# Queries and keys projected as features by tokens, and constants of the late loads derived past the values

## The chip, the cores and the metric

One core of one Trainium2 chip runs the whole block: TensorE (PE) multiplies into PSUM, VectorE (DVE) and the scalar engine (ACT) compute on SBUF and PSUM, GpSimd (POOL) on SBUF alone, and DMAs are issued from the queues of SyncE (SP) and ACT. The metric is device time in microseconds (us).

## The reference

A hybrid decoder block on x of 512 tokens by 1024. The part that matters here:

```python
xn = _rms_norm(h, mix_norm[l])
proj = xn @ w_in[l]                    # q, k, v, indexer, RWKV and gate columns
q = _rms_norm(q.reshape(B, S, 8, 64), attn_q_norm[l])
k = _rms_norm(k.reshape(B, S, 8, 64), attn_k_norm[l])
# sparse attention, by blocks of 128 queries:
scores = einsum(relu(einsum(q_idx, k_idx)), w_idx)       # then causal mask
_, sel = lax.top_k(scores, 128)
logits = einsum(q, k[sel]) * 64 ** -0.5 + rel_bias[bucket(q_pos - sel)]
y_attn = softmax(logits) @ v[sel]
```

Beside it run an RWKV-7 branch on other columns of the same projection, two gates, an output projection and a SwiGLU channel mixer.

## The kernel before

Every weight matrix comes in as one stream of chunks of 128x1024, 512 KB each, in the order of use. `chunk` (L233) loads one from SP's queue (w_raw, 2 buffers), ACT rounds it to the matmul's format (w_hi, L241, 3 buffers) and the rest, raw - hi, is made by GpSimd, or for every third chunk from number 17 on by VectorE (w_lo, L245, 3 buffers). A dense product is three matmuls (hi x hi, hi x lo, lo x hi), so that it keeps float32's precision.

`products` is the dense work from the first projection to the end: indexer's keys and queries, then queries, keys and values, RWKV's columns, gates, output, channel mixer. In its middle:

```python
for gain, name in ((qg, "q"), (pc("kn"), "k")):
    for g in range(2):
        yield from dense_k(xn, lambda t, ps: head_rms(g, gain, name, t, ps))
```

`dense_k` gives tokens by features: 128 tokens x 256 columns (four heads) to a product of 256 columns, two token blocks to a PSUM bank (ps_d, 3 banks). `head_rms` takes one such block out of PSUM (qraw), squares it (both ACT), sums by head (L449), adds epsilon (L450, both VectorE), raises to -1/2 on GpSimd (qrs, L452) and multiplies (L453, VectorE). Its `rest`, 14.5 modelled us later, flips the block to features by tokens (ps_i, 2 banks, L169) and takes it out as a high half (ACT, L464) and a low half (VectorE, L465): queries have the high half of a head on 64 partitions and the low half on the other 64 of one tile (qs_); keys have the high half twice (kh_, L467) and the low half twice (kl_, L468), so that two matmuls give the logits.

While that runs, VectorE does the indexer: `scores` (24 score products, ps_c, 3 banks; relu on ACT, weighted sum L416 and L420) and `select`, which finds the 128 largest scores of a row in 16 rounds of eight for each of three query blocks (L432 finds the maxima, L433 removes them, L435 makes the mask). `attention` starts when the values are there (vt, L966); for each of 32 units (4 query blocks x 8 heads) it makes logits (L523 to L533), their exponential (ACT, L534), flips them, and multiplies by the values.

The order on TensorE is the order in which the program is written. `Streams` sets it: each part is a generator, `mm` and `flip` advance a clock by a modelled time, a part yields how long it wants to wait (the table L), and the part of lowest rank that is due goes on; the dense work has the last rank. The other engines' order is chosen by the compiler's scheduler from dependences and its own model of time. In every engine, what waits holds back all that is queued behind it.

`derive` (L358) makes small constants on VectorE after the first projection is written: multiples of parameters, rkb (from con, which is loaded late from SP's queue), and eye16 and lev1 (from level1_t, loaded late too), which only the RWKV branch reads.

## Time and profile before

| | |
|---|---|
| Time, median of 3 runs (range) | 963.98 us (963.55 to 964.72) |
| The profiled execution's own time, and its span | 964.03 us, 962.2 us |
| Mean granted clock of TensorE over the span | 0.978 |
| TensorE busy, and weight loads | 915.0 us (95%), 779.0 us (81%) |
| VectorE, scalar engine, GpSimd busy | 435.9 (45%), 350.6 (36%), 372.3 us (39%) |
| Chain that ended last, by engine | PE 84%, DVE 11%, issue 2%, ACT 1%, POOL 1% |
| HBM read, written | 74.53 MB, 2.38 MB |

Times in the rows below count from the span's start. Matmuls are pipelined: the time from the start of one to the start of the next is its pace, and its own duration is longer. A busy share over the whole span is a mean over stages that have different limits.

### The profile page before, as it was taken

Reading aid. Unit: us, or ns where it says so; the run is one execution under the profiler, and the core shown is the slowest. Engines: PE = TensorE matmul, PEld = TensorE weight load, DVE = VectorE, ACT = ScalarE, POOL = GpSimd, SP = SyncE. Lnnn points to the kernel's source line nnn. Section 1 sums busy time; section 2 is a strip of 40 time slices with the busy share of each in tenths; the row PEclk is TensorE's granted clock in tenths of the full one; section 3 lists DMA queues with packets and bytes.
Section 4 is the critical chain, followed back from the end, with each engine's and each line's share of the span. In section 5 each row is a group of like instructions: output and inputs, shape, how many; then the busy total and the mean of one; then the engine's idle time right before and its main releaser. Section 6 shows DMA issues by size and latency. Waiting matters only on the chain.

```text
span 962.2 us, 13991 instructions
## 1 busy us (share of the span) xinstructions
PE 915.0 (95%) x5670; PEld 779.0 (81%) x5670; DVE 435.9 (45%) x847; ACT 350.6 (36%) x596; POOL 372.3 (39%) x253
## 2 busy tenths in 40 slices
PE   6998777999999999999997999999999999999998
PEld 4997776888777778787886899888888888888886
DVE  5289999677466635765533715211111111101111
ACT  5454466544453433333323424332232323212120
POOL 6445441101357334444413733344444444432321
PEclk9998888999998999999998999999999999999999
DMA  6321232211212121011042222332223323223331
GB/s 230 80 89 44 67 88 66 66 45 44 77 45 66 44 81 53 24 45 44 23 143 77 88 88 69 95 100 88 99 98 92 106 88 110 88 95 102 132 110 44
DMA packets 24033, 77.80 MB, mean 81 GB/s; under 512 B 2726, under 2 KB 4223, under 8 KB 23969
## 3 DMA queue, kind: packets, MB, share of 16 engines
q1 hardware_dynamic: 20832, 72.56, 23.4%
q10 hardware_dynamic: 3136, 4.36, 1.6%
q8 instruction: 44, 0.72, 0.3%
q14 instruction: 21, 0.16, 0.1%
HBM read 74.53 MB, written 2.38 MB: 80 GB/s over the span
## 4 chain that ended last, share of the span: by engine, by line
PE 84%; DVE 11%; issue 2%; ACT 1%; POOL 1%; DMA 0%; ACTq 0%; DVEq 0%; POOLq 0%
PE ps_d L162 60%; PE ps_c L162 11%; PE ps_i L162 10%; DVE score L433 2%; PE ps_c L169 2%; DVE max L432 2%; DVE qraw L453 1%; DVE score L420 1%; DVE qs L465 1%; PE ps_i L169 1%; DVE qss L449 1%; DVE lg L527 1%; POOL w_lo L245 0%; DVE kl L465 0%; DVE xs L330 0%
## 5 line engine op out<-in xcount | busy, mean ns | idle before, releaser
L245 POOL TENSOR_TENSOR w_lo<-w_raw,w_hi 128x1024 fp32r<-128x1024 f32 (+1 forms) x94 | 222.0, 2364 | 387.5 <-ACT w_hi L241 383.9
L241 ACT ACTIVATE w_hi<-w_raw 128x1024 fp32r<-128x1024 f32 x129 | 136.6, 1059 | 346.5 <-PE ps_d L162 219.4
L162 PE MATMUL ps_d<-hnl,w_hi 128*128 128x512 f32 (+1 forms) x368 | 139.9, 380 | 0.4 <-DVE hnl L338 0.4
L162 PE MATMUL ps_d<-hnh,w_hi 128*128 128x512 f32 (+1 forms) x368 | 139.9, 380 | 0.0
L162 PE MATMUL ps_d<-hnh,w_lo 128*128 128x512 f32 (+1 forms) x368 | 139.8, 380 | 0.0
L162 PE MATMUL ps_d<-xnh,w_hi 128*128 128x512 f32 (+2 forms) x296 | 124.5, 420 | 0.0
L162 PE MATMUL ps_d<-xnh,w_lo 128*128 128x512 f32 (+2 forms) x296 | 112.8, 381 | 0.0
L162 PE MATMUL ps_d<-xnl,w_hi 128*128 128x512 f32 (+2 forms) x296 | 112.4, 380 | 0.0
L245 DVE TENSOR_TENSOR w_lo<-w_raw,w_hi 128x1024 fp32r<-128x1024 f32 x37 | 47.6, 1286 | 126.8 <-ACT w_hi L241 126.2
L1045 DVE TENSOR_TENSOR gsig<-ps_d,gsig 128x512 f32<-128x512 f32 x22 | 15.2, 692 | 157.6 <-PE ps_d L162 156.9
L162 PEld LDWEIGHTS ps_d<-hnl,w_hi 128*128 128x128 f32 x368 | 69.2, 188 | 13.4 <-DVE hnl L338 0.6
L162 PEld LDWEIGHTS ps_d<-hnh,w_lo 128*128 128x128 f32 x368 | 69.2, 188 | 13.2
L162 PEld LDWEIGHTS ps_d<-hnh,w_hi 128*128 128x128 f32 x368 | 69.2, 188 | 13.2
L162 PEld LDWEIGHTS ps_d<-xnh,w_hi 128*128 128x128 f32 x296 | 57.2, 193 | 10.0 <-issue 2.6
L162 PEld LDWEIGHTS ps_d<-xnh,w_lo 128*128 128x128 f32 x296 | 56.8, 192 | 10.5
L162 PEld LDWEIGHTS ps_d<-xnl,w_hi 128*128 128x128 f32 x296 | 57.2, 193 | 8.1 <-issue 1.9
L162 PE MATMUL ps_d<-w_hi,xnh 128*128 128x256 f32 x192 | 58.9, 307 | 0.0
L162 PE MATMUL ps_d<-w_lo,xnh 128*128 128x256 f32 x192 | 57.7, 301 | 0.0
L162 PE MATMUL ps_d<-w_hi,xnl 128*128 128x256 f32 x192 | 57.6, 300 | 0.0
L1049 POOL TENSOR_TENSOR ul<-gsig,uh 128x512 fp32r<-128x512 f32 x22 | 31.6, 1434 | 25.3 <-ACT uh L1048 25.3
L162 PEld LDWEIGHTS ps_d<-w_hi,xnh 128*128 128x128 f32 x192 | 40.8, 212 | 0.4
L162 PEld LDWEIGHTS ps_d<-w_lo,xnh 128*128 128x128 f32 x192 | 40.5, 211 | 0.4
(283 smaller groups left out, 1814.9 us busy)
## 6 DMA issues: line engine op xcount, KB each, us to landing
w_raw<-in_stream_dram SPq DMA_DIRECT2D x129, 512.0 KB, 3.5
xa<-in_x_dram SPq DMA_DIRECT2D x4, 512.0 KB, 6.5
ht<-in_x_dram ACTq DMA_DIRECT2D x8, 256.0 KB, 3.2
out_dram<-ht SPq DMA_DIRECT2D x8, 256.0 KB, 2.0
toep<-bias_table ACTq DMA_DIRECT2D x8, 128.0 KB, 2.6
gain<-in_rows_dram ACTq DMA_DIRECT2D x2, 256.0 KB, 4.2
con<-in_consts_dram SPq DMA_DIRECT2D x1, 321.0 KB
bias_table<-tab ACTq DMA_DIRECT2D x1, 276.0 KB
```

Of the source, the lines that this page charges most:

```text
L162: nc.tensor.matmul(o, w, r, **kw)
L169: nc.tensor.transpose(o, src, idn)
L241: nc.scalar.activation(hi, raw, AF.Copy)
L245: eng.tensor_sub(lo[:, o:o + n_], raw[:, o:o + n_], hi[:, o:o + n_])
L420: nc.vector.scalar_tensor_tensor(sc, r, w, sc, op0=OP.mult, op1=OP.add)
L432: nc.vector.max(m8, sc)
L433: nc.vector.match_replace(sc, m8, sc, TAKEN)
L449: nc.vector.tensor_reduce(ss, hv(sq), axis=AX.X, op=OP.add)
L453: nc.vector.tensor_mul(hv(raw), hv(raw), rs[:, :, None].to_broadcast([128, 4, 64]))
L465: nc.vector.scalar_tensor_tensor(at_(lo, b), p2[a], gain[a], at_(hi, a), op0=OP.mult, op1=OP.subtract)
L1045: nc.vector.tensor_mul(g, pu, g)
L1049: nc.gpsimd.tensor_sub(ul, g, uh)
```

## The change

Queries and keys now come out of the projection as features by tokens: the weights stand still and 512 tokens pass, one product for two heads (`dense_t`, 24 matmuls of 512 columns each, four products for queries and four for keys; the weights' chunks and their order stay).

- Queries: `queries` squares the product out of PSUM (ACT) and splits it at once, unnormalised, by `split_heads`. The sum over a head's 64 features is now a sum over partitions: `head_sums` multiplies the squares by the two columns of blk, four matmuls to a bank of ps_i. After the fourth product two powers of 128x32 on GpSimd give every row's and head's scale (exponent -1/2) and its inverse, root (+1/2). Attention applies them: logits = q k + root x bias, masked, then the exponential with the scale as its factor. In the first block one fused add-and-maximum becomes two operations.
- Keys: `keys` copies the product with the gain to SBUF, sums as above, raises 128x8 on GpSimd, spreads the scales over 64 columns each (ACT), flips the spread tile on TensorE, multiplies keys by it and splits into high and low halves, both twice.
- `derive_more`, called after the values, holds what was the second part of `derive`; level1_t is loaded there, from ACT's queue.
- Attention waits for all queries and all keys at once, where it waited by block.

```diff
-L = dict(norm=3.0, normed=1.3, score=0.4, pick=0.15, rms=14.5, attn=0.6, ...
+L = dict(norm=3.0, normed=1.3, score=0.4, pick=0.15, rms=6.5, sums=2.5, attn=0.6, ...
...
-        nc.sync.dma_start(level1_t, consts[:, CONST_AT["level1_t"][0]:CONST_AT["level1_t"][1]])
...
+    half = cp.tile([128, 64], F32, name="half")
+    mhalf = half[:, 0:8]
+    nc.gpsimd.memset(half[:, 0:32], -0.5)
+    nc.gpsimd.memset(half[:, 32:64], 0.5)
...
+    def derive_more():
+        level1_t = unit("lv1t")[:, 0:128]
+        nc.scalar.dma_start(level1_t, consts[:, CONST_AT["level1_t"][0]:CONST_AT["level1_t"][1]])
         for p in range(4):
             nc.vector.tensor_scalar(rkb[:, p], cst("blk"), pc("r_k", p), None, op0=OP.mult)
         nc.vector.tensor_scalar(eye16, level1_t, 0.0, None, op0=OP.max)
...
-    def head_rms(g, gain, name, t, ps):
-        raw, sq = [q for q in unit("qraw").rearrange("q (a b) -> a q b", a=2)]
-        nc.scalar.activation(raw, ps, AF.Copy)
-        nc.scalar.activation(sq, raw, AF.Square, scale=N ** -0.5)
-        ss = small("qss", 4)
-        nc.vector.tensor_reduce(ss, hv(sq), axis=AX.X, op=OP.add)
-        nc.vector.tensor_scalar(ss, ss, RMS_EPS, None, op0=OP.add)
-        rs = small("qrs", 4)
-        nc.gpsimd.tensor_tensor(rs, ss, mhalf[:, 0:4], op=OP.pow)
-        nc.vector.tensor_mul(hv(raw), hv(raw), rs[:, :, None].to_broadcast([128, 4, 64]))
+    qss = cp.tile([128, NT, H], F32, name="qss")
+    qrs = cp.tile([128, 2, NT, H], F32, name="qrs")
+    def split_heads(j, src, gain, hi, lo, twice):
+        for e in range(2):
+            a, b, h = slice(64 * e, 64 * e + 64), slice(64 - 64 * e, 128 - 64 * e), 2 * j + e
+            if gain is None:
+                nc.scalar.activation(hi[a, h], src[a], AF.Copy)
+                nc.vector.tensor_sub(lo[b, h], src[a], hi[a, h])
+            else:
+                nc.scalar.activation(hi[a, h], src[a], AF.Copy, scale=gain[a])
+                nc.vector.scalar_tensor_tensor(lo[b, h], src[a], gain[a], hi[a, h], op0=OP.mult, op1=OP.subtract)
+            if twice:
+                nc.scalar.activation(hi[b, h], src[a], AF.Copy)
+                nc.scalar.activation(lo[a, h], lo[b, h], AF.Copy)
+    def head_sums(sq):
+        ps = bank("i")
+        for t in range(NT):
+            mm(ps[:, 2 * t:2 * t + 2], sq[:, t * 128:t * 128 + 128], cst("blk"), start=True, stop=True)
+        return ps[:, 0:8]
+    def queries(j, ps):
+        sq = unit("qsq")
+        nc.scalar.activation(sq, ps, AF.Square, scale=N ** -0.5)
+        split_heads(j, ps, qg, qs_, qs_, False)
         def rest():
+            s = head_sums(sq)
+            nc.vector.tensor_scalar(qss[:, :, 2 * j:2 * j + 2], s.rearrange("q (t h) -> q t h", h=2), RMS_EPS, None,
+                                    op0=OP.add)
+            if j == 3:
+                flat = lambda q: q.rearrange("q t h -> q (t h)")
+                for i in range(2):
+                    nc.gpsimd.tensor_tensor(flat(qrs[:, i]), flat(qss), half[:, i * 32:i * 32 + 32], op=OP.pow)
+                st.signal("q", 5.0)
+            yield 0.0
+        st.add(3, rest(), L["sums"])
+    def keys(j, ps):
+        raw, sq = unit("kraw"), unit("ksq")
+        nc.scalar.activation(sq, ps, AF.Square, scale=N ** -0.5)
+        nc.scalar.activation(raw, ps, AF.Copy, scale=pc("kn"))
+        def rest():
+            s = head_sums(sq)
+            ss, rs = small("qss", 8), small("qrs", 8)
+            nc.vector.tensor_scalar(ss, s, RMS_EPS, None, op0=OP.add)
+            nc.gpsimd.tensor_tensor(rs, ss, mhalf, op=OP.pow)
+            nc.scalar.activation(hv(sq), rs[:, :, None].to_broadcast([128, 8, 64]), AF.Copy)
+            yield L["rms"]
             ps = bank("i")
-            for j in range(2):
-                flip(ps[:, j * 128:j * 128 + 128], raw[:, j * 128:j * 128 + 128], ident)
-            p2 = ps[:, 0:256].rearrange("q (j t) -> q j t", j=2)
-            for e in range(2):
-                a, b = slice(64 * e, 64 * e + 64), slice(64 - 64 * e, 128 - 64 * e)
-                at_ = lambda z, q: pairs(z)[q, 2 * g:2 * g + 2, e, t * 128:t * 128 + 128]
-                hi, lo = (qs_, qs_) if name == "q" else (kh_, kl_)
-                nc.scalar.activation(at_(hi, a), p2[a], AF.Copy, scale=gain[a])
-                nc.vector.scalar_tensor_tensor(at_(lo, b), p2[a], gain[a], at_(hi, a), op0=OP.mult, op1=OP.subtract)
-                if name == "k":
-                    nc.scalar.activation(at_(hi, b), p2[a], AF.Copy, scale=gain[a])
-                    nc.scalar.activation(at_(lo, a), at_(lo, b), AF.Copy)
-            if g == 1:
-                st.signal(f"{name}{t}", 1.0)
+            for t in range(NT):
+                flip(ps[:, t * 128:t * 128 + 128], sq[:, t * 128:t * 128 + 128], ident)
+            nc.vector.tensor_mul(raw, raw, ps)
+            split_heads(j, raw, None, kh_, kl_, True)
+            if j == 3:
+                st.signal("k", 4.0)
             yield 0.0
-        st.add(3, rest(), L["rms"])
+        st.add(3, rest(), L["sums"])
...
+        yield "q"
+        yield "k"
...
+        scale, root = [qrs[:, j, i, h:h + 1] for j in range(2)]
         if i == 0:
-            nc.vector.tensor_tensor_reduce(lg, ps, toep[h][:, 128:256], 1.0, NEG, op0=OP.add, op1=OP.max,
-                                           accum_out=mx[:, 0:1])
+            nc.vector.scalar_tensor_tensor(lg, toep[h][:, 128:256], root, ps, op0=OP.mult, op1=OP.add)
+            nc.vector.tensor_reduce(mx[:, 0:1], lg, axis=AX.X, op=OP.max)
         else:
-            nc.vector.tensor_add(lg[:, n - 256:], ps[:, n - 256:], toep[h])
+            nc.vector.scalar_tensor_tensor(lg[:, n - 256:], toep[h], root, ps[:, n - 256:], op0=OP.mult, op1=OP.add)
             nc.vector.tensor_tensor_reduce(lg[:, n - 256:], lg[:, n - 256:], keep[i][:, n - 256:], 1.0, 2 * NEG,
                                            op0=OP.add, op1=OP.max, accum_out=mx[:, 0:1])
             if i > 1:
                 nc.vector.tensor_tensor_reduce(lg[:, :n - 256], ps[:, :n - 256], keep[i][:, :n - 256], 1.0,
                                                mx[:, 0:1], op0=OP.add, op1=OP.max, accum_out=mx[:, 1:2])
         m = mx[:, 1:2] if i > 1 else mx[:, 0:1]
-        nc.vector.tensor_scalar(mx[:, 2:3], m, -1.0, None, op0=OP.mult)
-        nc.scalar.activation(lg, lg, AF.Exp, bias=mx[:, 2:3], accum_out=den[:, h:h + 1])
+        nc.vector.tensor_scalar(mx[:, 2:3], m, scale, -1.0, op0=OP.mult, op1=OP.mult)
+        nc.scalar.activation(lg, lg, AF.Exp, scale=scale, bias=mx[:, 2:3], accum_out=den[:, h:h + 1])
...
-        for gain, name in ((qg, "q"), (pc("kn"), "k")):
-            for g in range(2):
-                yield from dense_k(xn, lambda t, ps: head_rms(g, gain, name, t, ps))
+        for part in (queries, keys):
+            for j in range(4):
+                if j % 2 == 0:
+                    wt = chunk(4, 256) + chunk(4, 256)
+                ps = bank("d")
+                yield from dense_t(ps, wt, slice((j % 2) * 128, (j % 2) * 128 + 128), xn)
+                part(j, ps)
         for g in range(2):
             yield from dense_k(xn, lambda t, ps: nc.scalar.activation(vt[t][:, g * 256:g * 256 + 256], ps, AF.Copy))
         st.signal("v", 1.0)
+        derive_more()
```

The order of GpSimd's instructions in the stage (qrs are the powers for queries and keys, w_lo the low parts of weight chunks). Before:

```order
L452 TENSOR_TENSOR qrs<-qss,mhalf 128x4 x2
L245 TENSOR_TENSOR w_lo<-w_raw,w_hi 128x1024
L452 TENSOR_TENSOR qrs<-qss,mhalf 128x4 x2
L245 TENSOR_TENSOR w_lo<-w_raw,w_hi 128x1024
L452 TENSOR_TENSOR qrs<-qss,mhalf 128x4 x2
L245 TENSOR_TENSOR w_lo<-w_raw,w_hi 128x1024 x8
```

Now, from the chunks ahead of the keys' last one to those behind the last key's power:

```order
L244 TENSOR_TENSOR w_lo<-w_raw,w_hi 128x1024 x10
L484 TENSOR_TENSOR qrs<-qss,half 128x32 x2
L244 TENSOR_TENSOR w_lo<-w_raw,w_hi 128x1024
L499 TENSOR_TENSOR qrs<-qss,half 128x8
L244 TENSOR_TENSOR w_lo<-w_raw,w_hi 128x1024
L499 TENSOR_TENSOR qrs<-qss,half 128x8 x2
L244 TENSOR_TENSOR w_lo<-w_raw,w_hi 128x1024 x2
L499 TENSOR_TENSOR qrs<-qss,half 128x8
L244 TENSOR_TENSOR w_lo<-w_raw,w_hi 128x1024 x8
```

Pairs of short powers alternated with chunks; now two wide powers stand in one piece ahead of the low part of the keys' last chunk and of the keys' own powers.

TensorE in the third product of the keys (con,ksq are the sums over a head, fst,ksq the flips of the spread scales of the first two heads, ps_d the dense product), with what it waits for; there is no such place before:

```order
L162 MATMUL ps_i<-con,ksq 128x2 [waits Activation_49]
L162 MATMUL ps_i<-con,ksq 128x2 x3
L162 MATMUL ps_d<-xnh,w_hi 128x512
L162 MATMUL ps_d<-xnl,w_hi 128x512
L162 MATMUL ps_d<-xnh,w_lo 128x512 [waits Pool_49]
L162 MATMUL ps_d<-xnh,w_hi 128x512
L162 MATMUL ps_d<-xnl,w_hi 128x512
L162 MATMUL ps_d<-xnh,w_lo 128x512
L169 MATMUL ps_i<-fst,ksq 128x128 [waits DVE_49,Activation_49]
L169 MATMUL ps_i<-fst,ksq 128x128 x3
```

The wait on Pool is that for the low part of the keys' last chunk, which stands behind the two wide powers; all of attention, and the values, come later on TensorE.

VectorE at the start, around the constants (xs and xnl belong to the first norm). Before:

```order
L365 TENSOR_SCALAR eye_124<-lv1t 128x128
L367 CAST lev_126<-lv1t 128x128
L364 TENSOR_SCALAR rkb<-con,fst 128x2 x4
L338 TENSOR_TENSOR xnl<-ps_i,xnh 128x4x128 x2
L330 SCALAR_TENSOR_TENSOR xs<-xa,ss,ps_c 128x512 x2
```

Now:

```order
L367 TENSOR_SCALAR rkb<-con,fst 128x2 x4
L337 TENSOR_TENSOR xnl<-ps_i,xnh 128x4x128 x2
L329 SCALAR_TENSOR_TENSOR xs<-xa,ss,ps_c 128x512 x2
L337 TENSOR_TENSOR xnl<-ps_i,xnh 128x4x128 x4
L983 TENSOR_TENSOR kil<-ps_d,kih 64x512
```

The two conversions of level1_t have left this place (they stand among the keys now); the four rkb rows stand where they stood. From the first product of attention on, TensorE's order is the same in both but for two places where like products are grouped in another way.

## Rows read from the trace of the kernel before

**Rows 1.** Busy time by stretches: from the first column of the span, the stretch (us from the start) and its length, then for TensorE, its weight loads, VectorE (DVE), the scalar engine (ACT) and GpSimd (POOL) the busy us and in brackets the instructions; then the granted clock of TensorE as a share of full speed (PEclk), the DMA engines' busy share and GB/s. One stretch of 25 us; the stretch from VectorE's first score row to its first attention row; and the 100 us after TensorE's first attention product.

```profile
125.00:150.00 25.00, 15.78 (x106) 14.79 (x106) 23.98 (x52) 17.64 (x39) 6.39 (x4) 0.83 0.28 83
48.77:162.74 113.97, 91.74 (x648) 88.31 (x647) 107.36 (x246) 63.36 (x138) 42.18 (x27) 0.88 0.23 69
162.34:262.00 99.66, 97.97 (x570) 82.84 (x569) 69.16 (x216) 47.01 (x109) 21.87 (x14) 1.00 0.18 56
```

**Rows 2.** Who TensorE waited for, longest in total: us, times, the longest.

```profile
PE ps_i L169 <- ACT kh L467: 11.6, 4, 4.9
PE ps_i L169 <- DVE qs L465: 10.0, 3, 5.4
```

**Rows 3.** The same columns as in rows 1, in stretches of 2 us after one of these waits.

```profile
80.00:82.00 2.00, 0.00 (x0) 0.00 (x0) 1.90 (x5) 0.88 (x2) 0.00 (x0) 1.00 0.00 0
84.00:86.00 2.00, 1.35 (x6) 0.98 (x6) 1.90 (x8) 1.58 (x5) 0.65 (x1) 0.50 0.00 0
90.00:92.00 2.00, 2.00 (x17) 2.00 (x16) 1.90 (x6) 0.47 (x1) 1.01 (x1) 0.92 0.62 166
```

**Rows 4.** TensorE's instructions in order of time: start, us, engine, line, what is written from what, tiles and count. The first and the twelfth product of the queries; four flips of queries and the product after them; two products of 512 columns of the next projection; the first product of attention's logits; the first flip of attention's probabilities; four column sums of the other branch (two records for each) and the product after them.

```profile
46.51 0.28 PE L162 MATMUL ps_d<-w_hi,xnh 128*128 128x256 f32 x1
47.81 0.28 PE L162 MATMUL ps_d<-w_hi,xnl 128*128 128x256 f32 x1
75.43 0.60 PE L169 MATMUL ps_i<-fst,qraw 128*128 128x128 f32 x4
75.78 0.36 PE L162 MATMUL ps_d<-w_hi,xnh 128*128 128x256 f32 x1
161.65 0.40 PE L162 MATMUL ps_d<-xnh,w_hi 128*128 128x512 f32 x1
161.88 0.39 PE L162 MATMUL ps_d<-xnl,w_hi 128*128 128x512 f32 x1
162.34 0.22 PE L162 MATMUL ps_c<-kh,qs 128*128 128x128 f32 x1
165.53 0.27 PE L169 MATMUL ps_c<-fst,lg 128*128 128x128 f32 x1
269.83 0.95 PE L162 MATMUL ps_i<-con,sq 128*128 128x2 f32 x8
270.64 0.49 PE L162 MATMUL ps_d<-xnh,w_hi 128*128 128x512 f32 x1
```

**Rows 5.** VectorE's instructions from 48.77 to 162.74 us, grouped by line and shape: count, busy us, mean ns of one, idle time before them.

```profile
L453 DVE TENSOR_TENSOR qraw<-qraw,qrs 128x256 f32<-128x256 f32 x16 | 17.4, 1090 | 0.1
L465 DVE SCALAR_TENSOR_TENSOR qs<-ps_i,der,qs 64x256 fp32r<-64x256 f32 x16 | 7.6, 483 | 0.5
L465 DVE SCALAR_TENSOR_TENSOR kl<-ps_i,fst,kh 64x256 fp32r<-64x256 f32 x16 | 7.6, 483 | 0.9 <-ACT kh L464 0.3
L449 DVE TENSOR_REDUCE qss<-qraw 128x4 f32<-128x256 f32 x16 | 6.3, 410 | 0.0
L450 DVE TENSOR_SCALAR qss<-qss 128x4 f32<-128x4 f32 x16 | 2.2, 162 | 0.1
L435 DVE TENSOR_SCALAR score<-score 128x384 f32<-128x384 f32 x1 | 2.1, 2084 | 0.0
```

**Rows 6.** The same view of VectorE from 160 to 310 us.

```profile
L389 DVE SCALAR_TENSOR_TENSOR zk<-ps_d,der,zk 128x511 f32<-128x511 f32 x4 | 3.0, 744 | 0.0
L664 DVE TENSOR_TENSOR kr<-zr,dec 128x512 f32<-128x512 f32 x4 | 2.7, 678 | 0.2
```

**Rows 7.** Instructions in order of time, of VectorE and of GpSimd: a multiplication of queries alone and one beside a w_lo, and the end of the first selection beside two powers of queries.

```profile
73.01 0.41 DVE L453 TENSOR_TENSOR qraw<-qraw,qrs 128x256 f32<-128x256 f32 x1
74.33 2.61 DVE L453 TENSOR_TENSOR qraw<-qraw,qrs 128x256 f32<-128x256 f32 x1
74.26 2.40 POOL L245 TENSOR_TENSOR w_lo<-w_raw,w_hi 128x1024 fp32r<-128x1024 f32 x1
101.95 0.28 DVE L435 TENSOR_SCALAR score<-score 128x256 f32<-128x256 f32 x1
101.19 1.98 POOL L452 TENSOR_TENSOR qrs<-qss,mhalf 128x4 f32<-128x4 f32 x2 [4.31 <-DVE qss L450]
```

**Rows 8.** GpSimd's instructions of the whole span, grouped by line and shape, columns as in rows 5: the low parts of weights, and powers of 1, 4 and 8 columns.

```profile
L245 POOL TENSOR_TENSOR w_lo<-w_raw,w_hi 128x1024 fp32r<-128x1024 f32 x90 | 216.8, 2410 | 385.9 <-ACT w_hi L241 382.4 <-issue 3.4
L328 POOL TENSOR_TENSOR ss<-ss,mhalf 128x1 f32<-128x1 f32 x8 | 4.4, 555 | 14.5 <-DVE ss L327 12.7 <-DVE ss L323 1.8
L452 POOL TENSOR_TENSOR qrs<-qss,mhalf 128x4 f32<-128x4 f32 x16 | 17.1, 1083 | 30.7 <-DVE qss L450 30.7
L647 POOL TENSOR_TENSOR krs<-kss,mhalf 128x8 f32<-128x8 f32 x4 | 8.9, 2225 | 4.4 <-DVE kss L645 4.4
L884 POOL TENSOR_TENSOR yrs<-yst,mhalf 128x8 f32<-128x8 f32 x4 | 6.6, 1641 | 5.2 <-DVE yst L882 5.2
```

**Rows 9.** VectorE in order of time: the search for maxima that begins round 15 of the first selection, and the first logits of attention.

```profile
98.58 0.43 DVE L432 MAX8 max<-score 128x8 f32<-128x256 f32 x1
162.74 0.29 DVE L523 CUSTOM_DVE_ANT_0 lg<-ps_c,toep 128x128 f32<-128x128 f32 x1
```

**Rows 10.** VectorE in order of time at the start: one of the two conversions of level1_t, and the four rows of rkb.

```profile
13.02 0.22 DVE L365 TENSOR_SCALAR eye<-lv1t 128x128 f16<-128x128 f32 x1
13.28 2.72 DVE L364 TENSOR_SCALAR rkb<-con,fst 128x2 f32<-128x2 f32 x4
```

More of the change, by code (lines that the diff above doesn't have):

```diff
@@ L34 @@
 UA = ("score", "relu", "widx_t", "tab", "ytile", "sg", "ag", "wa2", "seg", "am", "u32", "ht")
-SMALL = {"ss": 4, "max8": 3, "qss": 4, "qrs": 4, "mx": 4}
+SMALL = {"ss": 4, "max8": 3, "mx": 4}
 def shape_constants():
@@ L85 @@
     NPAR += _c
-L = dict(norm=3.0, normed=1.3, score=0.4, pick=0.15, rms=14.5, attn=0.6, attn_n=0.15, attn_out=2.0, sig=0.3,
+L = dict(norm=3.0, normed=1.3, score=0.4, pick=0.15, rms=6.5, sums=2.5, attn=0.6, attn_n=0.15, attn_out=2.0, sig=0.3,
          prep=5.0, knorm=6.5, bonus=6.0, mat=0.5, mats=2.8, inv_u=3.25, inv_t=1.4, inv_r=1.4, inv_n=0.9, inv_e=1.8,
@@ L210, in hybrid_block @@
     nc.gpsimd.memset(rel, 1.0)
-    level1_t = unit("lv1t")[:, 0:128]
     def load_rest():
-        nc.sync.dma_start(level1_t, consts[:, CONST_AT["level1_t"][0]:CONST_AT["level1_t"][1]])
         nc.sync.dma_start(con, consts[:, 0:nc_])
@@ L226, in pc @@
         return par[lo:hi, PAR_AT[name] + j:PAR_AT[name] + j + 1]
-    mhalf = cp.tile([128, 8], F32, name="mhalf")
-    nc.gpsimd.memset(mhalf, -0.5)
+    half = cp.tile([128, 64], F32, name="half")
+    mhalf = half[:, 0:8]
+    nc.gpsimd.memset(half[:, 0:32], -0.5)
+    nc.gpsimd.memset(half[:, 32:64], 0.5)
     at = [0]
@@ L497, in attention @@
                 if h == 0:
-                    yield f"q{i}"
-                    yield f"k{i}"
                     if i:
```

1 line of the change is left out of this document (removed).

## The prediction

> **What bounds the kernel now.** I read the busy shares first: TensorE is busy 95% of the span, no other engine half of it. Such a kernel gets shorter where TensorE has less to do or waits, so the question is where it waits and for whom. The table by stretches answers that [rows 1]: from 125 to 150 us TensorE is busy 15.78 us of 25, VectorE 23.98, and the granted clock is 0.83. That is the stage of the queries, keys and values: TensorE starts its first queries' product at 46.51 and its first attention product at 162.34 [rows 4], 115.8 us later. From there to 262 us TensorE is busy 97.97 of 99.66 us at clock 1.00. So this stage is bound by VectorE (107.36 busy of 113.97 us), the next by TensorE; what the first loses or gains moves all that follows.
>
> TensorE's waits name the place: 11.6 + 10.0 us before the flips of normalised queries and keys (ps_i, L169), until the low and high halves of the flip before have been taken out [rows 2]. The clock adds to it: TensorE stands still from 80 to 82 us, then runs at 0.50 of full speed, 1.2 of 2.4 GHz, at 84 to 86 us, and at a mean of 0.92 from 90 to 92 [rows 3]. TensorE's own work in the stage is 576 products of 256 columns at 0.12 us [rows 4], 48 score products (16 each of 256, 384 and 512 columns, 8.3 us by the same pace), 32 flips and 6 products of 512 columns, some 82 us; the other 34 of the 115.8 are waiting and slow clock.
>
> **The change part by part.**
>
> *TensorE.* 384 products of 256 columns at 0.12 us (eleven from 46.51 to 47.81) become 192 of 512 at 0.23 us (161.65 to 161.88) [rows 4]: 46.1 against 44.2 us. The values stay, 192 x 0.12 = 23.0. Flips go from 32 to 16, at 0.35 us per four (75.43 to 75.78) [rows 4]: 1.4 us are left. Eight column sums come in; the nearest row is the like product of the other branch, ps_i<-con,sq, at 0.81 us for four (269.83 to 270.64) [rows 4]: +6.5. With 8.3 us of score products and 1.4 of the next projection it comes to 84.8, so TensorE gets 3 us more and would reach attention at 131.3 if it never waited. It saves nothing here by itself.
>
> *VectorE.* Out go, in the stage: 16 multiplications by the row's power, 17.4 us; 32 low halves, 7.6 + 7.6; 16 reductions, 6.3; 16 additions of epsilon, 2.2: 41.1 us [rows 5]. In come: 8 low halves of queries, 64x512 out of PSUM with a scalar, taken at the 0.744 of L389 (511 columns, same operands): 6.0; 4 multiplications of keys with a PSUM operand at the 0.678 of L664, which has both in SBUF: 2.7; 8 subtractions of keys' low halves at the same: 5.4 [rows 6]; 8 epsilons at 0.162 [rows 5]: 1.3; two constants, 0.22 each as they were at 13.02 [rows 10]: 0.4. That is 15.8, net -25.3.
>
> Not all of it comes back. The multiplications that go took 1.09 us in the mean, though one alone takes 0.41 (at 73.01 [rows 7]), because of w_lo on GpSimd: one that began at 74.33 lasted 2.61 us, to just after the end of a w_lo that ran from 74.26 for 2.40. A w_lo blocks whatever two-operand VectorE work comes first behind its start. Those multiplications took much of the blow: 17.4 less 16 x 0.41 is 10.8 us. The w_lo stay, and the score sums (relu and score, both in SBUF) and the new keys' subtractions will take some of it: between 0 (they miss each other) and 11 us (all are hit); I take 6, since score sums stand at every second place while four of the w_lo run and the search for maxima, which was not blocked, fills the rest. Fewer independent neighbours between the dependent steps of the search cost another 2 (0 to 4). So VectorE reaches the first attention row, 162.74 [rows 9], 25.3 - 8 = 17.3 us earlier, at 145.4; bounds 10 and 25.
>
> *GpSimd, and TensorE behind it.* 16 powers of 128x4 go. In come four of 128x8 for the keys and, in one piece after the fourth query, two of 128x32 [order of GpSimd]. The trace has none of 32 columns: 0.555, 1.083, 1.641 and 2.225 us for 1, 4, 8 and 8 [rows 8], and two of 4 in 1.98 where nothing stood beside them [rows 7]. By the step from 0.99 to 1.641, 0.16 a column, one takes 5.4; by that from 0.555 to the slower 8, 0.24, it takes 8.0. The pair is 10.8 to 16 us; I take 10.8, since the 0.99 was taken on these very numbers. Behind it in GpSimd's queue stand the low part of the last keys' weights and then each key's power. The pair starts when VectorE has done the fourth epsilon, four places ahead of the end of the first selection. Before, round 15 of that selection began at 98.58 [rows 9]; half of what goes out (20.5) and seven eighths of the queries' work (5.9) lie ahead of it, net -14.6, and 4 to 7 for blocking, so about 90. Then: pair until 101, w_lo (2.41, [rows 8]) until 103.4, first key's power until 105, copy and flip at about 106. TensorE by its own sum stands at that w_lo from some 96: it waits 7 us, and 1.7 more for the flip. Behind lie four flips of four (1.4), 27 products (6.2), two sums (1.6), the values (23.0) and six products (1.4), 33.6 us, so it comes to attention at about 139.6, or 143 if the clock falls as it did after 80 us, and to the first flip of attention 3.2 us on, as before (162.34 to 165.53) [rows 4]: 142.8 to 146.3. VectorE, 2.8 us from its first attention row to that flip (162.74 to 165.53), allows it at 148.2. The two are close; VectorE is the later.
>
> *Scalar engine.* It was busy 63.36 of 113.97 us [rows 1] and loses more instructions than it gains; its work and the copy that spreads keys' powers lie beside VectorE's.
>
> *Attention.* The bias is now multiplied by the root (one operation for one), and eight units of the first block get one reduction more, some 0.25 us by the half of L449's 0.410. VectorE is busy 69.16 of 99.66 us there [rows 1], so 2 to 4 us of work are mostly hidden; I charge 0.7 (0 to 3).
>
> *Constants.* Two 128x128 conversions and one load leave the start. But the four rkb rows stand at the same place in VectorE's order; they took 2.72 us from 13.28 there [rows 10], beside two halves of a w_lo, and still will. I put this at 0 (-0.3 to 0). That part of the title does little.
>
> A rule of the skill speaks against the wide powers. A plain one-input tensor_scalar ran 0.28 us at 101.95 in the middle of a power that lasted from 101.19 for 1.98 [rows 7]: powers did not block it, where w_lo blocked a like one of 384 columns for 2.1 us [rows 5]. The Trainium skill, "SBUF — State Buffer", section "Who interferes with whom", says that a two-port VectorE instruction and a GpSimd instruction exclude each other for the whole instruction, whichever they are. By the rows the powers cost VectorE nothing; by that rule they cost what the rival "powers that block" below has. For the powers the trace disagrees; for w_lo it agrees.
>
> **Sum.** Before, the first flip of attention was at 165.53 [rows 4]; now 148.2: -17.3. Attention +0.7, and 0.6 for a clock that may fall when TensorE waits for that flip. All behind is in the same order on TensorE. The profiled execution took 964.03 us (span 962.2 and 1.8 around it), level with the median, 963.98. 964.0 - 16.0 = **948.0 us**.
>
> **Rivals.**
> - *Forecast*, 943 to 951: chance 0.60.
> - *The pair of powers sets the end.* At 16 us instead of 10.8 TensorE is at that flip 5.2 later, 148 to 151.5. VectorE's key multiplications and later sums wait for flips that come 5 us later, of which it has 1 to 2 us in hand, so VectorE too loses 3 to 5: the flip is at 151 to 153.5, and 9 to 12 us are gained: 952 to 955, say **954**. For it: nothing is known of 32 columns; against: the 0.99. Chance 0.17.
> - *Nothing new is blocked* (0 instead of 6). Then VectorE is at attention by 139.4, the flip could be at 142.2, and the pair's own path is last, at 142.8: 22.7 gained, less 0.7: **942**. Against: score sums are dense. Chance 0.13; TensorE unhindered (131.3, or 934) would need VectorE earlier still and is its far end.
> - *Powers that block.* If VectorE's end of the first selection, some four steps behind the fourth epsilon, has to wait for the pair, 7 us go: **955**. Against: 0.28 at 101.95. Chance 0.03.
> - *Slower: wide powers far dearer by the column.* Each us of the pair beyond some 13 moves attention by one. From 10.8 to no gain it needs 19 us more, 30 for the pair, 0.47 a column, twice the dearest step in rows 8; at 0.6 a column, **972**. Chance 0.04 slower, and 0.03 that it ends level (0.03: same).
>
> **How the numbers follow.** Faster by over 0.2%, about what a measurement here can tell from no change, 0.60 + 0.17 + 0.13 + 0.03 = 0.93; within, 0.03; slower, 0.04. The range takes the forecast's own, most of the second case and half of the third: 940 to 957.
>
> **What would show it.** Right: first flip of attention between 144 and 153; TensorE's waits at ps_i nearly gone, one wait of 6 to 12 us on w_lo in the keys in their place; two powers of 5 to 6 us; VectorE still over 90% busy from 75 us to attention; score sums of 2 us and more beside w_lo; rkb at 13 to 16 us as before. Wrong: powers of 8 us or more (second rival), score sums undisturbed (third), TensorE waiting in attention where it did not (the 0.7 was too small), or the whole after attention not merely shifted.

## The result and the profile after

The changed kernel takes 947.92 us (median of 4 runs, 946.07 to 948.31) against 963.76 for the kernel before on the same chip: a ratio of 0.9833, with a 95% interval of 0.9815 to 0.9851. Its profiled execution took 946.07 us, span 943.9. The forecast was 948.0.

Some executions of most kernels here, the one before too, took some 8 to 15 us more, lost behind 290 us of the span at a lower granted clock (0.88 to 0.89 from 290 to 400 us in three profiles, 0.97 to 1.00 in the rest), so the times below are medians of the others (column "used") and profiles are compared ahead of that place only. Even the executions that are used differ by 1 to 6 us for one kernel, so a difference of 1 us between two kernels is not settled.

The table by stretches of the changed kernel: columns as in rows 1. The first stretch is again from VectorE's first score row to its first attention row, the next two are the 50 us in which TensorE waits and its clock falls, the last is attention.

```profile
47.56:143.13 95.57, 89.59 (x516) 78.80 (x516) 90.23 (x201) 54.28 (x90) 44.05 (x18) 0.95 0.27 83
75.00:100.00 25.00, 21.92 (x113) 18.26 (x111) 23.99 (x65) 9.13 (x13) 17.84 (x5) 0.96 0.14 42
100.00:125.00 25.00, 23.23 (x130) 20.52 (x131) 24.27 (x52) 15.67 (x25) 13.81 (x8) 0.83 0.41 130
141.73:241.40 99.67, 95.50 (x559) 80.52 (x558) 70.87 (x210) 47.97 (x107) 19.50 (x14) 1.00 0.19 56
```

The stage is 18.4 us shorter than in [rows 1] (95.57 for 113.97), and VectorE is still busy 94% of it. TensorE's waits from 45 to 146 us, columns as in [rows 2]:

```profile
PE ps_d L162 <- POOL w_lo L244: 3.4, 1, 3.4
PE ps_i L162 <- ACT ksq L492: 1.3, 1, 1.3
PE ps_c L162 <- DVE score L419: 1.1, 1, 1.1
PE ps_c L169 <- ACT lg L573: 0.9, 1, 0.9
```

The 21.6 us at the flips are gone; one wait behind GpSimd has come in, as announced, 3.4 us long and not 7. Its place in order of time, GpSimd first and then TensorE, with the first products of attention and its first flip:

```profile
87.13 10.84 POOL L484 TENSOR_TENSOR qrs<-qss,half 128x32 f32<-128x32 f32 x2 [3.69 <-DVE qss L479]
97.94 2.35 POOL L244 TENSOR_TENSOR w_lo<-w_raw,w_hi 128x1024 fp32r<-128x1024 f32 x1
100.24 1.64 POOL L499 TENSOR_TENSOR qrs<-qss,half 128x8 f32<-128x8 f32 x1
...
96.52 0.40 PE L162 MATMUL ps_d<-xnl,w_hi 128*128 128x512 f32 x1
...
100.34 0.80 PE L162 MATMUL ps_d<-xnh,w_lo 128*128 128x512 f32 x1 [3.42 <-POOL w_lo L244]
...
102.59 1.12 PE L169 MATMUL ps_i<-fst,ksq 128*128 128x128 f32 x4 [0.18 <-ACT ksq L500]
...
141.73 0.22 PE L162 MATMUL ps_c<-kh,qs 128*128 128x128 f32 x1
...
145.96 0.33 PE L169 MATMUL ps_c<-fst,lg 128*128 128x128 f32 x1 [0.88 <-ACT lg L573]
```

The pair takes 10.84 us, w_lo behind it lands at 100.3, TensorE has stood since 96.9 and goes on at a lower clock (0.50 of full speed, 1.2 of 2.4 GHz, from 100 to 104 us, a mean of 0.83 from 100 to 125). It still comes to attention at 141.73; VectorE, whose first row there starts at 143.13 without idle time before it, is the later one:

```profile
12.99 2.77 DVE L367 TENSOR_SCALAR rkb<-con,fst 128x2 f32<-128x2 f32 x4
...
77.73 0.74 DVE L459 SCALAR_TENSOR_TENSOR qs<-ps_d,der,qs 64x512 fp32r<-64x512 f32 x1
...
78.84 1.25 DVE L425 TENSOR_TENSOR score<-score,con 128x128 f32<-128x128 f32 x1
...
90.57 0.28 DVE L438 TENSOR_SCALAR score<-score 128x256 f32<-128x256 f32 x1
...
143.13 0.33 DVE L562 SCALAR_TENSOR_TENSOR lg<-toep,qrs,ps_c 128x128 f32<-128x128 f32 x1
```

The rkb rows stand where they stood [rows 10]. The low half of queries at 77.73 ran its plain 0.74 us inside a w_lo (from 77.37 for 2.58), and the addition with both operands in SBUF behind it was held until that w_lo ended at 79.95. The row of 0.28 at 90.57 stands inside the pair of powers. VectorE's groups in the stage, columns as in [rows 5]:

```profile
L423 DVE SCALAR_TENSOR_TENSOR score<-relu,widx,score 128x384 f32<-128x384 f32 x7 | 7.6, 1081 | 0.0
L456 DVE TENSOR_TENSOR kl<-kraw,kh 64x512 fp32r<-64x512 f32 x8 | 7.4, 919 | 0.3
L459 DVE SCALAR_TENSOR_TENSOR qs<-ps_d,der,qs 64x512 fp32r<-64x512 f32 x8 | 6.0, 750 | 1.1 <-ACT qs L458 0.9
...
L505 DVE TENSOR_TENSOR kraw<-kraw,ps_i 128x512 f32<-128x512 f32 x4 | 2.7, 677 | 0.0
...
L479 DVE TENSOR_SCALAR qss<-ps_i 128x8 f32<-128x8 f32 x4 | 0.6, 160 | 0.1
```

### The profile page after: what moved, and what is told of

It is laid out like the page before. It is cut to its first block, busy times and chain, and to the rows that moved or that the text cites. A ratio compares the mean times of both kernels' runs of the same rounds, so it can differ in the third digit from the quotient of the medians.

```text
span 943.9 us, 13579 instructions
## 1 busy us (share of the span) xinstructions
PE 909.3 (96%) x5526; PEld 764.8 (81%) x5526; DVE 419.5 (44%) x795; ACT 344.0 (36%) x548; POOL 373.0 (40%) x244
## 4 chain that ended last, share of the span: by engine, by line
PE 82%; DVE 11%; issue 2%; ACT 2%; POOL 2%; DMA 0%; ACTq 0%; POOLq 0%; DVEq 0%
PE ps_d L162 59%; PE ps_c L162 11%; PE ps_i L162 9%; DVE score L436 2%; DVE max L435 2%; PE ps_c L169 2%; DVE score L423 1%; DVE lg L566 1%; POOL w_lo L244 1%; DVE qs L459 1%; PE ps_i L169 0%; PE ps_d L169 0%; DVE xs L329 0%; DVE kl L456 0%; DMA grow<-in_rows_dram 0%
## 5 line engine op out<-in xcount | busy, mean ns | idle before, releaser
L162 PE MATMUL ps_d<-xnh,w_hi 128*128 128x512 f32 (+2 forms) x360 | 149.7, 416 | 0.0
L162 PE MATMUL ps_d<-xnh,w_lo 128*128 128x512 f32 (+2 forms) x360 | 137.8, 383 | 3.4 <-POOL w_lo L244 3.4
L162 PE MATMUL ps_d<-xnl,w_hi 128*128 128x512 f32 (+2 forms) x360 | 136.8, 380 | 0.0
L162 PEld LDWEIGHTS ps_d<-xnh,w_hi 128*128 128x128 f32 x360 | 68.8, 191 | 11.4 <-issue 2.6
L162 PEld LDWEIGHTS ps_d<-xnl,w_hi 128*128 128x128 f32 x360 | 68.9, 192 | 9.8 <-issue 1.9
L1093 POOL TENSOR_TENSOR ul<-gsig,uh 128x512 fp32r<-128x512 f32 x22 | 31.6, 1435 | 25.3 <-ACT uh L1092 18.0
L798 POOL COPY rr<-eye 128x512 f16<-128x512 f16 x20 | 15.5, 780 | 47.9 <-PE ps_i L162 47.9
L162 PE MATMUL ps_d<-w_hi,mh 128*128 128x256 f32 x120 | 34.1, 284 | 0.0
L162 PE MATMUL ps_d<-w_hi,ml 128*128 128x256 f32 x120 | 34.0, 283 | 0.0
L162 PE MATMUL ps_d<-w_lo,mh 128*128 128x256 f32 x120 | 34.0, 283 | 0.0
L573 ACT ACTIVATE lg<-lg,mx,qrs 128x128 f32<-128x128 f32 (+3 forms) x32 | 20.8, 651 | 32.1 <-DVE mx L572 31.2
```

The source lines that it names most:

```text
L162: nc.tensor.matmul(o, w, r, **kw)
L573: nc.scalar.activation(lg, lg, AF.Exp, scale=scale, bias=mx[:, 2:3], accum_out=den[:, h:h + 1])
L798: nc.gpsimd.tensor_copy(two(R, 1), eye16.rearrange("q (g w s) -> q g w s", w=2, s=s)[:, None, :, 1] .to_broadcast([128, H, 64 // s, s]))
L1093: nc.gpsimd.tensor_sub(ul, g, uh)
```

## The experiments

All are edits of the changed kernel, and some also give VectorE another order, which the compiler chooses: 12 to 16 steps of the third selection stand ahead of attention's first row. The table sums them up: where the stage starts (first score product), attention's first logits and first flip of probabilities, the stage's length (flip less start), attention's length (first flip to the next product behind it, zwa), all from the trace; then the time, and how many of the executions it is the median of. A flip 3.2 us behind the logits means that VectorE was ready for them; where it comes further behind, VectorE was the later of the two engines.

| | start | logits | flip | stage | attention | time | used |
|---|---|---|---|---|---|---|---|
| before | 47.93 | 162.34 | 165.53 | 117.60 | 91.86 | 963.8 | 4 of 4 |
| changed | 46.69 | 141.73 | 145.96 | 99.27 | 94.27 | 947.9 | 4 of 4 |
| again | 46.77 | 143.06 | 147.25 | 100.48 | 94.26 | 948.0 (with the 4 above) | 5 of 6 |
| const_early | 46.79 | 141.84 | 145.62 | 98.83 | 94.34 | 946.9 | 5 of 6 |
| root_product | 48.03 | 141.26 | 145.69 | 97.66 | 94.90 | 946.9 | 6 of 6 |
| pair_twice | 47.13 | 155.51 | 158.70 | 111.57 | 94.19 | 958.2 | 7 of 10 |
| queries_only | 47.24 | 147.16 | 151.22 | 103.98 | 94.52 | 953.3 | 5 of 10 |
| keys_only | 48.13 | 150.77 | 153.97 | 105.84 | 91.87 | 951.7 | 3 of 4 |
| relu_psum | 47.33 | 137.28 | 142.27 | 94.94 | 94.26 | 944.2 | 5 of 6 |
| all_psum | 47.14 | 136.56 | 139.75 | 92.61 | 94.47 | 940.3 | 4 of 6 |
| psum_root | 47.10 | 133.62 | 136.81 | 89.71 | 95.10 | 939.4 | 3 of 6 |
| fused_block | 47.92 | 144.21 | 147.40 | 99.48 | 93.81 | 948.0 | 4 of 6 |
| rkb_late | 45.43 | 141.72 | 145.24 | 99.81 | 94.70 | 944.8 | 4 of 6 |
| best | 45.44 | 132.08 | 135.27 | 89.83 | 95.08 | 937.7 | 6 of 6 |

**Again**, without an edit.

> The changed kernel once more. In its first profiled execution attention's first flip came 19.6 us earlier than before, 1.2 of them already at the start of the stage, and 18.3 were left at the end, while the medians differ by 15.8. If the terms are stable: median 947 to 948.5, first flip at 145.5 to 146.5, attention giving back about 2.4. If the profiled execution (946.07) was only a lucky one: the same first flip and about 2 us more lost behind it.

The terms are stable: attention again gives back 2.4, the stage is 17.1 shorter than before (18.3 in the first profile). The start, which nothing had touched, stood at 46.7 to 47.3 in most profiles and at 47.9 to 48.1 in three of the edits and in the kernel before, so the 1.2 us are not the change's. They arise mostly at one place: eight flips of the first norm, at about 20 us. The changed kernel, and the kernel before:

```profile
19.95 1.03 PE L169 MATMUL ps_i<-fst,xs 128*128 128x128 f32 x8
```

```profile
20.34 1.88 PE L169 MATMUL ps_i<-fst,xs 128*128 128x128 f32 x8
```

All profiles that start at 47.9 or later have 1.9 us there, the others 1.0 to 1.3: the flips run still at the slower of TensorE's two paces or already at the faster one, though the granted clock is given as 1.00 in both.

**Const_early.**

```diff
+    level1_t = unit("lv1t")[:, 0:128]
+
     def load_rest():
         nc.sync.dma_start(con, consts[:, 0:nc_])
+        nc.sync.dma_start(level1_t, consts[:, CONST_AT["level1_t"][0]:CONST_AT["level1_t"][1]])
...
     def derive_more():
-        level1_t = unit("lv1t")[:, 0:128]
-        nc.scalar.dma_start(level1_t, consts[:, CONST_AT["level1_t"][0]:CONST_AT["level1_t"][1]])
...
         derive()
+        derive_more()
...
         st.signal("v", 1.0)
-        derive_more()
```

> The constants of the late loads made where they were before, all else as in the changed kernel. Theory (the prediction's, constants worth 0): within 0.3 us of the changed kernel. Rival (the trace of the changed kernel, in which the stage starts 1.2 us earlier): the first score product at about 47.9 instead of 46.7, and 0.5 to 1.2 us slower than the changed kernel.

46.79 and 946.9: the constants' move is worth nothing. The rival, read from one pair of traces, falls.

**Root_product and pair_twice.**

```diff
-                for i in range(2):
-                    nc.gpsimd.tensor_tensor(flat(qrs[:, i]), flat(qss), half[:, i * 32:i * 32 + 32], op=OP.pow)
+                nc.gpsimd.tensor_tensor(flat(qrs[:, 0]), flat(qss), half[:, 0:32], op=OP.pow)
+                nc.gpsimd.tensor_mul(flat(qrs[:, 1]), flat(qrs[:, 0]), flat(qss))
```

> The second wide power (root) replaced by a multiplication of scale with the sum on GpSimd. Theory (VectorE's own row of work ends the stage): TensorE's 3.4 us wait for the last keys' w_lo goes with the slow clock behind it, but attention's first flip moves by less than 1 us; 0 to 1 us faster than the changed kernel. Rival (the pair of powers sets the end): 3.4 to 5 us faster.

> The same two 128x32 powers a second time right behind the first, into a tile that nobody reads: 10.9 us more on GpSimd ahead of the last keys' w_lo. Theory (TensorE came to attention only 1.4 us ahead of VectorE's first row there, so the pair has hardly more cover): TensorE waits about 14 us instead of 3.4, and attention comes 8 to 11 us later; 956 to 959. Rival (GpSimd is far from the path): 0 to 2 us.

GpSimd with the root as a product, in order of time:

```profile
89.73 5.43 POOL L483 TENSOR_TENSOR qrs<-qss,half 128x32 f32<-128x32 f32 x1 [3.52 <-DVE qss L479]
95.24 0.25 POOL L484 TENSOR_TENSOR qrs<-qrs,qss 128x32 f32<-128x32 f32 x1
95.45 2.40 POOL L244 TENSOR_TENSOR w_lo<-w_raw,w_hi 128x1024 fp32r<-128x1024 f32 x1
```

5.2 us less on GpSimd, no wait on w_lo left, and yet the stage is only 1.2 to 2.8 us shorter and the time 1.1: VectorE is the later engine here too (the flip comes 4.4 us behind the logits). The test is not a clean one. In this kernel's order VectorE has 5.2 us less to do ahead of attention, three steps of the third selection among it, and idles some 3.5 us more: 1.7 for TensorE and 2.0 for a load that `derive_more` brought here:

```profile
118.38 0.52 DVE L368 TENSOR_SCALAR eye<-lv1t 128x128 f16<-128x128 f32 x1 [1.97 <-DMA lv1t<-in_consts_dram]
```

So it shows that the pair does not cost its whole length, and leaves open whether it costs 1 us or 3. With the pair twice, GpSimd, TensorE's longest wait, and VectorE's first row of attention:

```profile
88.80 10.84 POOL L485 TENSOR_TENSOR qrs<-qss,half 128x32 f32<-128x32 f32 x2 [3.52 <-DVE qss L480]
99.60 10.82 POOL L487 TENSOR_TENSOR qxx<-qss,half 128x32 f32<-128x32 f32 x2
```

```profile
PE ps_d L162 <- POOL w_lo L244: 14.0, 1, 14.0
```

```profile
155.88 0.35 DVE L565 SCALAR_TENSOR_TENSOR lg<-toep,qrs,ps_c 128x128 f32<-128x128 f32 x1 [4.87 <-PE ps_c L162]
```

10.8 us more there make the stage 11.1 to 12.7 us longer, and the time 10; now VectorE waits for TensorE. Upward the pair has hardly any cover: in the changed kernel VectorE was the later by about 1 us (4.2 us from logits to flip against 3.2).

**Queries_only and keys_only.** The one part as changed, the other by `dense_k` and `head_rms` as before; with the keys alone attention is as before.

```diff
-        for part in (queries, keys):
+        for part in (queries,):
...
+        for g in range(2):
+            yield from dense_k(xn, lambda t, ps: head_rms(g, pc("kn"), "k", t, ps))
```

> Queries as in the changed kernel, keys as before (tokens by features, flips). Theory (the stage is bound by VectorE's sum of work): of the net 25.3 us that the sum takes from VectorE the queries have 8 x (1.09 + 0.483 + 0.410 + 0.162) x ... = 20.5 out and 6.65 in, 13.9; with the same share of it coming back as in the whole change (17.3 of 25.3) 9.5 us, less 2.4 that attention gives back: 956 to 958. Rival (what counts is TensorE's stalls at the flips with the slow clock behind them, of which queries and keys have two each): 10 us of stalls and some 6 of slow clock go, 949 to 951.

> Keys as in the changed kernel, queries as before, and attention as before (no root, no scale in the exponential, the fused first block). Theory: 20.5 us out of VectorE, 8.8 in (four multiplications, eight subtractions, four epsilons), 11.7; by the same share 8.0 us gained, nothing lost in attention: 955 to 957. Rival (stalls at the flips): 11.6 us of stalls and some 5 of slow clock go, 947 to 950.

Neither theory held: 953.3 and 951.7 lie between the two forecasts. The stage is 13.6 us shorter with the queries alone and 11.8 with the keys alone, which is the whole of my net sums (13.9, 11.7) without the share that I had taken off. Together they would be 25.4, and the change, again and const_early have 17.1 to 18.8. Attention's length is 91.87 with the keys alone, as before, so its 2.4 us come from the queries' scales. VectorE in the stage with the keys alone:

```profile
L526 DVE TENSOR_TENSOR qraw<-qraw,hrs 128x256 f32<-128x256 f32 x8 | 7.4, 923 | 0.0
L456 DVE TENSOR_TENSOR kl<-kraw,kh 64x512 fp32r<-64x512 f32 x8 | 5.5, 686 | 0.3
...
L423 DVE SCALAR_TENSOR_TENSOR score<-relu,widx,score 128x384 f32<-128x384 f32 x7 | 4.3, 608 | 0.0
```

The queries' multiplications still take the blow of w_lo there (0.92 for 0.41), and the score sums of 384 columns and the keys' subtractions are at their plain price; in the whole change these two take it (1.08 and 0.92). The score sums take it with the queries alone already:

```profile
L423 DVE SCALAR_TENSOR_TENSOR score<-relu,widx,score 128x384 f32<-128x384 f32 x7 | 7.6, 1080 | 0.0
```

Why the two do not add up can be counted on VectorE, row by row, from its first score row to its first attention row. What rows last above the price of the same row undisturbed sums to 14.4 us before, 8.2 with the queries alone, 10.0 with the keys alone and 7.4 in the change: alone they save 6.2 and 4.5 of it, together only 7.1. And the search for maxima ahead of attention lasts 52.6 us before, 53.3 and 51.1 alone, 54.8 in the change, where the order puts two more steps of the third selection there. Its maxima before and in the change:

```profile
L432 DVE MAX8 max<-score 128x8 f32<-128x512 f32 x13 | 9.0, 692 | 0.3
```

```profile
L435 DVE MAX8 max<-score 128x8 f32<-128x512 f32 x15 | 10.4, 691 | 0.3
```

The first makes 3.6 us of the difference, the second 3.0.

**Relu_psum, psum_root, all_psum.** Three edits in steps: relu in its PSUM bank; with it the keys' product in PSUM (all_psum); with both, the root as a product (psum_root).

```diff
-                    r = unit("relu")[:, :n]
-                    nc.scalar.activation(r, ps, AF.Relu)
-                    nc.vector.scalar_tensor_tensor(sc, r, w, sc, op0=OP.mult, op1=OP.add)
+                    nc.scalar.activation(ps, ps, AF.Relu)
+                    nc.vector.scalar_tensor_tensor(sc, ps, w, sc, op0=OP.mult, op1=OP.add)
...
-            nc.vector.tensor_mul(raw, raw, ps)
-            split_heads(j, raw, None, kh_, kl_, True)
+            nc.vector.tensor_mul(ps, raw, ps)
+            split_heads(j, ps, None, kh_, kl_, True)
```

> The changed kernel with the score's relu written back into its PSUM bank, so that the weighted sum has one operand in PSUM and one in SBUF. Theory (w_lo on GpSimd blocks the next VectorE instruction that has two operands in SBUF, and one with a PSUM operand goes through, as the low half of queries of 0.74 us at 77.73 did inside the w_lo that ran from 77.37 for 2.58): no score sum over 0.8 us; VectorE comes to attention 1.5 to 3 us earlier, TensorE, then last, leaves 0.5 to 1.5 us of it. Rival (such a sum is blocked as well): no change within 0.3 us; or the three ps_c banks, now held until VectorE is done, cost 1 us or more.

> The changed kernel with three edits together: relu in PSUM, the keys' normalised product written back into its PSUM bank (so that the low halves of keys have a PSUM operand too), and the second wide power replaced by a multiplication. Theory (VectorE's blocked time and the pair of powers are the two things close to the end of the stage): attention's first flip 3 to 5 us earlier than in the changed kernel, 943 to 945.5. Rival (one of the two ps_i banks held for the keys stops the next sums): within 1 us of the changed kernel or slower.

> The changed kernel with relu in PSUM and the keys' product in PSUM, the pair of wide powers kept. It tells apart what the three edits together (938.3 to 940.4) have beyond relu in PSUM alone (942.8 to 944.8). Theory: once VectorE is relieved, the pair of powers on GpSimd is the next bound (the rival of the prediction, one step further on): 942 to 944.5, with a first flip of keys near 99.4 as with relu in PSUM alone. Rival: it is the keys' subtractions, 0.91 us beside w_lo and 0.69 alone, 1.9 us, and the pair is worth nothing: 938 to 940.5.

VectorE's groups with relu in PSUM alone, and then with all three edits:

```profile
L455 DVE TENSOR_TENSOR kl<-kraw,kh 64x512 fp32r<-64x512 f32 x8 | 7.3, 912 | 0.2
...
L422 DVE SCALAR_TENSOR_TENSOR score<-ps_c,widx,score 128x384 f32<-128x384 f32 x7 | 4.3, 610 | 0.1
```

```profile
L455 DVE TENSOR_TENSOR kl<-ps_i,kh 64x512 fp32r<-64x512 f32 x8 | 5.5, 688 | 0.3
...
L422 DVE SCALAR_TENSOR_TENSOR score<-ps_c,widx,score 128x384 f32<-128x384 f32 x7 | 4.3, 608 | 0.1
```

No sum is blocked with its operand in PSUM (0.61 for 1.08), then no subtraction either (0.69 for 0.92). In all_psum two of these sums and three of the subtractions begin inside a w_lo and run at their plain price (0.60 and 0.69); in the changed kernel two sums that begin inside one took 2.17 and 2.36, one subtraction 2.55. (With the keys alone and in root_product no subtraction begins inside one.) The gain was larger than expected: 3.9 us for relu, 7.7 with the keys, 8.6 with the root. For all_psum the theory fell (940.3, not 942 to 944.5): the keys' product in PSUM is worth 3.9 by the medians, the pair some 1. By the traces the two are worth 2.3 and 2.9 of the stage, but with the root as a product two steps of the search, 2.1 us, have moved behind attention's first row; what each is worth stays open at this spread. That the blow is what was in the way is shown by all_psum: rows last 1.3 us above their plain price there, 7.4 in the changed kernel (8.6 again), and the stage is 6.2 to 7.9 us shorter than in the changed kernel, again and const_early. With all three, VectorE's and TensorE's shares of the stage:

```profile
47.97:133.99 86.02, 84.62 (x511) 74.99 (x511) 79.85 (x194) 53.50 (x90) 37.48 (x17) 1.00 0.32 93
```

TensorE is now busy 84.62 of 86.02 us at clock 1.00, so the stage has become TensorE's, and 1.4 us at most are left to be had from VectorE.

**Fused_block.** The first block's factor root on its bias is left out.

```diff
-            nc.vector.scalar_tensor_tensor(lg, toep[h][:, 128:256], root, ps, op0=OP.mult, op1=OP.add)
-            nc.vector.tensor_reduce(mx[:, 0:1], lg, axis=AX.X, op=OP.max)
+            nc.vector.tensor_tensor_reduce(lg, ps, toep[h][:, 128:256], 1.0, NEG, op0=OP.add, op1=OP.max, ...)
```

> The changed kernel with the first block's add and maximum as one operation again; the factor root on its bias is left out there. Attention took 94.3 us from its first flip to the next product behind it, before 91.9. Theory (the eight reductions and the longer start of a row are a part of it): 0.5 to 1.0 us of the 2.4 go. Rival (all of it is in the later blocks, where the row's longer operations meet w_lo): 94.3 as it is.

93.81: 0.5 us in the trace, nothing visible in the medians. Of the rest 1.2 us lie at one place late in attention, where TensorE's next logits wait (columns as in [rows 4]; the changed kernel, VectorE's row and TensorE's):

```profile
212.90 2.46 DVE L566 CUSTOM_DVE_ANT_0 lg<-lg,score 128x256 f32<-128x256 f32 x1
...
216.04 0.47 PE L162 MATMUL ps_c<-kh,qs 128*128 128x512 f32 x1 [0.98 <-DVE mx L569]
```

Before and with the keys alone a w_lo hits the same row (2.34 and 2.32 us), but TensorE does not wait there. Root_product and psum_root lose another 0.6 to 0.8 us right behind the first flip; why is not shown.

**Rkb_late and best.** Two columns loaded once more on the scalar engine's queue, behind level1_t, so that the rkb rows cannot run early; best adds it to the three edits above.

```diff
-        level1_t = unit("lv1t")[:, 0:128]
+        late = unit("lv1t")
+        level1_t, blk = late[:, 0:128], late[:, 128:130]
         nc.scalar.dma_start(level1_t, consts[:, CONST_AT["level1_t"][0]:CONST_AT["level1_t"][1]])
+        nc.scalar.dma_start(blk, consts[:, CONST_AT["blk"][0]:CONST_AT["blk"][1]])
         for p in range(4):
-            nc.vector.tensor_scalar(rkb[:, p], cst("blk"), pc("r_k", p), None, op0=OP.mult)
+            nc.vector.tensor_scalar(rkb[:, p], blk, pc("r_k", p), None, op0=OP.mult)
```

> The changed kernel with the two columns that rkb is made from loaded once more beside level1_t, so that the four rkb rows leave the start for the place behind the last load, which the change's words announce. They lasted 2.77 us from 12.99, between the first norm's rows. Theory: the last scale of the norm comes from GpSimd at 16.0, behind a w_lo, and xs stood at 16.88, so 0.5 to 0.9 us are gained at the start and at the end. Rival: all 2.8 us are; or nothing, since another row takes the place beside w_lo.

> The three edits together (relu and the keys' product in PSUM, root by a multiplication) and the late rkb: 938 to 939.5 where nothing but the sum of the two counts; within 0.5 us of the three edits if the start gives nothing.

TensorE's last-but-one group of flips in the first norm, in the changed kernel and with rkb late:

```profile
16.42 1.97 PE L169 MATMUL ps_i<-fst,xs 128*128 128x128 f32 x8 [3.29 <-DVE xnl L337]
```

```profile
14.55 1.97 PE L169 MATMUL ps_i<-fst,xs 128*128 128x128 f32 x8 [1.06 <-DVE xnl L337]
```

Those flips wait for xnl, which stood behind rkb and, with an operand in PSUM, now passes the w_lo that held rkb. They come 1.9 us earlier, and the stage starts at 45.4 in both kernels. The time falls by 1.7 in best against psum_root, where the end of attention too comes 1.6 earlier. In rkb_late it falls by 3.3 (median), but the end of attention comes only 0.3 to 1.6 earlier than in the changed kernel and again; the rest lies behind it and is not explained. The theory's 0.5 to 0.9 was too small: I had looked at xs alone. Best is at 937.66 us (935.68 to 939.09, 6 runs), 10 us below the changed kernel and 26 below the one before. The seven used executions of the kernel before that were taken beside it have a median of 962.21 us, a ratio of 0.974.

## Why the prediction was right, point by point

- **VectorE bounds the stage: right.** Its row of work became 18.4 us shorter in the first profile and 17.2 in the second (96.78 for 113.97); forecast 17.3. The durations of all its rows there sum to 116.3 us before and 96.0 after: 20.3 less, forecast 25.3 - 6 = 19.3. The overlap of neighbouring rows (durations and idle time together, less the stretch: 116.3 + 6.6 - 114.0, and 96.0 + 5.3 - 95.6) fell from 8.9 to 5.8, 3.1 for the forecast 2; idle time fell by 1.3.
- **w_lo passes from the multiplications to score sums and subtractions: right, and shown** by relu_psum and all_psum; **the size was not.** Hit in the changed kernel: score sums 3.3 us (7.6 less 7 x 0.61), subtractions 1.9 (7.4 less 8 x 0.69), one addition 1.0, one row with a single operand 1.2; the 256-column sums, hit for 2.0 before, are free now, and that single row was hit for 1.7. So 3.6 of the 10.7 us on the multiplications came back and not 6. In the sum this was made up by the 2.2 us of search that moved ahead of attention, which the forecast did not have: that 20.3 stands so near to 19.3 is in part luck. The Trainium skill, "SBUF — State Buffer", section "Who interferes with whom", says that a VectorE instruction with two SBUF inputs contends with a GpSimd instruction that reads SBUF, and one with at most one SBUF input, outside its two-port modes, doesn't: 1.08 us against 0.61 here. The trace agrees.
- **The pair of powers: price right (5.42 us each, forecast 5.4; worked out again, its step of 0.16 a column gives 5.5), place 3 us too late.** It started at 87.13 and not 90, and so everything on that path came 3 us earlier: w_lo at 100.3 for 103.4, the wait 3.4 for 7, the flip of keys at 102.6 for 106. TensorE at attention: 141.73, within 139.6 to 143, but by two misses that cancel: from that flip it took 39.1 us, where 33.6 were forecast, or 37.0 with the fall of the clock. It was busy for 37.9 of them at a mean clock of 0.92 and waited 1.3 for the squares of the last keys. That VectorE is the later of the two is shown by the 4.2 us from logits to flip; that they are close, by pair_twice. The point beyond which the pair moves attention, which I put at some 13 us, is by that about 12.
- **Rivals.** The pair at 16 us fell with its price. Powers that block fell with the 0.28 us at 90.57. "Nothing new is blocked" did not happen by itself, but all_psum makes it happen: a stage 25.0 us shorter, the net sum, and 940.3 us, forecast 942. Its far end, TensorE unhindered (131.3, or 934), was approached by psum_root: 133.6 and 939.4.
- **Attention: the term that was mis-sized.** 0.7 + 0.6 was forecast and 2.4 measured in the changed kernel, inside the bounds of 0 to 3; the kernels that scale there have 2.0 to 3.2. 0.5 is the first block, 1.2 a wait behind one w_lo.
- **Constants: right at 0** (const_early), for the reason given: rkb stays. The step done as its words say would have been worth some 1.7 us by best against psum_root.
- **Sum.** Stage -18.1 (mean of the first profile, again and const_early, 99.5 for 117.6) and attention +2.4 make -15.7, the medians differ by 15.8, forecast -16.0. The stage was forecast 0.8 too short of its gain and attention 1.1 too cheap; the exact hit owes something to that. It owes something to the spread as well: the three profiled executions took 17.8 to 18.3 us less than that of before, 1.2 of it by the start and 1 to 2 behind attention, where the forecast had nothing.

What stays open: what the pair alone is worth, since root_product moved the search and brought a wait for a load, and why TensorE's way from the last flip of keys to attention took 2 us more than the forecast with the slow clock.
